# A decoder layer with 32 experts: the second product of each run worked among the pieces of the next run's first product, and pairs of experts on whole float32 weights

## The chip, the cores and the metric

The kernel runs on one NeuronCore of a Trainium2 chip. The metric is the device time of one execution in microseconds (us). Before the change it is 1546.03 us, the median of three runs (1543.41 to 1550.98). The engines are TensorE (PE; its weight loads are a row of their own, PEld), VectorE (DVE), ScalarE (ACT), GpSimd (POOL) and SyncE (SP), which issues the loads.

## The reference

One decoder layer on 512 tokens of width 1024: a mixer with two head groups, then a mixture of experts, then a per-layer embedding and a norm. The change concerns the experts alone. Every token goes to 4 of 32 experts; an expert takes the rows given to it through two products with a clamped, gated activation between them, and the results are summed per token by their gates.

```python
hh = jnp.dot(xs, w_gu[e]) + b_gu[e]              # (rows, 1024) x (1024, 2048)
glu, lin = jnp.split(hh, 2, axis=-1)
glu = jnp.minimum(glu, SWIGLU_LIMIT)
lin = jnp.clip(lin, -SWIGLU_LIMIT, SWIGLU_LIMIT)
act = glu * jax.nn.sigmoid(SWIGLU_ALPHA * glu) * (lin + 1.0)
return jnp.dot(act, w_dn[e]) + b_dn[e]           # (rows, 1024) x (1024, 1024)
```

All weights are float32. An expert's weights are 12 MB, those of all 32 are 384 MB, and each is read once.

## The kernel before

**Tiling.** The experts are sorted by the number of their tokens, the fullest first, and each rank has a fixed number of slots (CAPS): 128 for ranks 0 to 4, then 112, 96, 80 and 72, and 64 for the last twelve. Ranks 0 to 19 are worked alone (a single), ranks 20 to 31 two at a time (a pair; the two experts lie in the two 64-column halves of the PE array). RUNS is the order: run 0 is rank 0, runs 1 and 2 are pairs, 3 to 5 singles, 6 a pair, 7 to 10 singles, 11 a pair, 12 to 17 singles, 18 a pair, 19 to 24 singles, and 25 (LAST) a pair.

**Pieces.** An expert's weights are cut into 12 pieces of 1 MB (128 partitions x 2 x 1024 float32). Pieces 0 to 7 are the first product's (w_gu: 0 to 3 the gate half, 4 to 7 the linear half), 8 to 11 the second's (w_dn). The list jobs holds all pieces in the order of their use. SyncE loads them in this order into RAW, a ring of eight slots (issue, raw_slot, L770). A slot comes free again when its piece has been split or, for a piece used as it is, when PE has used it (done).

**Split and native pieces.** A split writes a piece as two float16 parts into HL, a ring of six slots: ScalarE writes the high part (L212, `hl<-raw`), VectorE the low part (L213). PE then takes three float16 products for one (mm3, L218 to L220). NATIVE says how many of an expert's last pieces are not split but multiplied in float32 straight from the raw slot: 4 for a rank with 64 slots (its second product), 0 for the others. advance runs the splits AHEAD = 4 places of the list ahead of the piece that PE takes.

**A run.** prep builds the one-hot matrix of the run's tokens and gather collects their columns on PE into xT (L1242, copied by ScalarE in L1244). up is the first product: for each half a bias product (L1276), then the pieces, then the activation (L1295 to L1300: glu, ln). In a pair, up runs once for each expert, each with 64 token columns. After up, prep of the next run; then down_t (or down for 128 slots, down2 for a pair: L1361) is the second product, into the PSUM tiles yT or y. y_out scales y by the gates into yh and yl (L1371, L1372). After every third run a combine adds three runs' results to the tokens (L1383, and acc in L1385); it is a generator that up works off a step at a time.

So in program order all of a run's first product comes first, then all of its second, and the next run starts behind it. A scheduler moves single instructions a little; the order that each engine really has is shown in the section on the change.

## Time and profile before

| what | value |
|---|---|
| median of three runs | 1546.03 us |
| the profiled execution | 1546.58 us |
| its span in the trace | 1544.8 us |
| PE busy | 1349.7 us, 87% |
| VectorE busy | 1216.5 us, 79% |
| ScalarE busy | 1012.2 us, 66% |
| bytes moved | 433.27 MB, 280 GB/s over the span |

The busy times are those of the profiled execution. The ends of products on PE are modelled by the profiler, so a PE that is shown busy need not be working at its full pace; the distance between the starts of products tells more. The page cuts the span into 40 slices of 38.6 us; the expert part begins in the ninth and ends in the thirty-ninth. The granted clock is a share of TensorE's 2.4 GHz.

### The profile page before, as it was taken

What the parts mean: (1) busy time and instruction counts of PE and PEld (TensorE: products, weight loads), DVE (VectorE), ACT (ScalarE), POOL (GpSimd) and SP (SyncE); (2) the same over time, 40 slices, a digit from 0 to 9 for tenths busy, and PEclk for the clock granted to TensorE, in tenths of its full rate; (3) what the DMA queues carried; (4) which work ended last, traced back from release to release, by engine and by line L of the source; (5) the groups of instructions that cost most, each with busy time, mean ns of one, the idle gap of its engine ahead of it and who ended that gap; (6) DMA issues with size and microseconds to landing.
All of it is one profiled execution on the core that took longest, in us unless ns stands there. A gap on an engine that the chain in (4) does not pass through costs nothing. (4 is left out here: it accounts for less than half of the span.)

```text
span 1544.8 us, 48662 instructions
## 1 busy us (share of the span) xinstructions
PE 1349.7 (87%) x21678; PEld 1060.3 (69%) x21678; DVE 1216.5 (79%) x1356; ACT 1012.2 (66%) x1156; POOL 49.2 (3%) x114
## 2 busy tenths in 40 slices
PE   7999899878889999899998899988887788798687
PEld 4766656466665787777797578878765777667447
DVE  7447876688595998769999299999975899988834
ACT  6458765557373777558688177777844767867634
POOL 2001000210000000000000000000000000000002
PEclk9999999879999999999999999999999999999799
DMA  7122130358999999889989789999997999998911
GB/s 244 51 86 83 56 110 29 110 188 276 340 379 364 410 408 336 312 321 408 391 308 380 269 325 408 395 340 374 352 328 278 408 381 343 311 350 289 359 66 56
DMA packets 124264, 433.27 MB, mean 280 GB/s; under 512 B 7977, under 2 KB 18770, under 8 KB 123986
## 3 DMA queue, kind: packets, MB, share of 16 engines
q1 hardware_dynamic: 123858, 429.85, 75.5%
q8 instruction: 171, 2.80, 0.7%
q14 instruction: 43, 0.35, 0.1%
q10 hardware_dynamic: 192, 0.26, 0.1%
HBM read 427.99 MB, written 2.10 MB: 278 GB/s over the span
## 5 line engine op out<-in xcount | busy, mean ns | idle before, releaser
L213 DVE SCALAR_TENSOR_TENSOR hl<-raw,hl 128x2048 f16<-128x2048 f32 x337 | 762.9, 2287 | 77.5 <-ACT hl L212 76.2
L212 ACT ACTIVATE hl<-raw 128x2048 f16<-128x2048 f32 x337 | 630.0, 1903 | 129.4 <-DMA raw<-in_w_gu_dram 57.8
L220 PE MATMUL hps<-xT,hl 128*128 128x64 f16 (+5 forms) x4096 | 493.4, 204 | 49.6 <-DVE hl L213 40.3
L218 PE MATMUL hps<-xT,hl 128*128 128x64 f16 (+5 forms) x4096 | 497.4, 204 | 12.5 <-issue 7.2
L219 PE MATMUL hps<-xT,hl 128*128 128x64 f16 (+5 forms) x4096 | 496.9, 204 | 8.6 <-issue 8.6
L220 PEld LDWEIGHTS <-hl 128*128 128x128 f16 (+1 forms) x4208 | 400.4, 100 | 76.0 <-DVE hl L213 53.6
L218 PEld LDWEIGHTS <-hl 128*128 128x128 f16 (+1 forms) x4208 | 403.0, 100 | 37.6 <-issue 10.8
L219 PEld LDWEIGHTS <-hl 128*128 128x128 f16 (+1 forms) x4208 | 403.1, 100 | 28.1 <-issue 12.0
L1342 PE MATMUL yT<-acts,hl 128*128 128x80 f16 (+3 forms) x960 | 120.7, 210 | 7.8 <-DVE acts L213 7.8
L1341 PE MATMUL yT<-acts,hl 128*128 128x80 f16 (+3 forms) x960 | 121.9, 209 | 1.7 <-ACT acts L212 1.6
L1343 PE MATMUL yT<-acts,hl 128*128 128x80 f16 (+3 forms) x960 | 120.6, 210 | 0.8 <-DVE hl L213 0.7
L1361 PE MATMUL y<-raw,ln 128*64 128x512 f32 x384 | 101.3, 611 | 11.4 <-DMA raw<-in_w_dn_dram 9.1
L1343 PEld LDWEIGHTS <-hl 128*128 128x128 f16 x960 | 98.2, 103 | 10.1 <-issue 8.9
L1341 PEld LDWEIGHTS <-hl 128*128 128x128 f16 x960 | 98.1, 103 | 3.2 <-issue 2.2
L1342 PEld LDWEIGHTS <-hl 128*128 128x128 f16 x960 | 98.4, 103 | 0.5 <-issue 0.3
L1372 DVE SCALAR_TENSOR_TENSOR yl<-y,gcl,yh 128x512 f16<-128x512 f32 (+4 forms) x52 | 37.7, 744 | 68.1 <-ACT yh L1371 67.5
L1383 PE MATMUL pg<-yh,ohT 128*128 128x512 f16 (+4 forms) x208 | 80.5, 389 | 10.5 <-issue 5.0
L1371 ACT ACTIVATE yh<-y,gcl 128x512 f16<-128x512 f32 (+4 forms) x52 | 35.0, 682 | 82.8 <-PE y L1361 71.0
L1244 ACT ACTIVATE xT<-pg 128x512 f16<-128x512 f32 (+4 forms) x104 | 51.7, 513 | 50.0 <-PE pg L1242 42.3
L1383 PE MATMUL pg<-yl,ohT 128*128 128x512 f16 (+4 forms) x208 | 80.7, 389 | 1.8 <-DVE yl L1372 1.7
L1361 PEld LDWEIGHTS y<-raw,ln 128*64 128x64 f32 x384 | 31.9, 139 | 67.5 <-issue 59.3
L1383 PEld LDWEIGHTS <-ohT 128*128 128x128 f16 (+4 forms) x416 | 38.5, 99 | 51.5 <-issue 23.4
(369 smaller groups left out, 2251.6 us busy)
## 6 DMA issues: line engine op xcount, KB each, us to landing
raw<-in_w_gu_dram SPq DMA_DIRECT2D x256, 1024.0 KB, 9.6
raw<-in_w_dn_dram SPq DMA_DIRECT2D x128, 1024.0 KB, 8.1
raw<-in_w_in_dram SPq DMA_DIRECT2D x2, 2048.0 KB
raw<-in_w_o_dram SPq DMA_DIRECT2D x2, 2048.0 KB
raw<-in_w_ple_gate_dram SPq DMA_DIRECT2D x4, 1024.0 KB
acc<-in_x_dram SPq DMA_DIRECT2D x4, 512.0 KB, 3.5
raw<-in_w_in_dram SPq DMA_DIRECT2D x4, 512.0 KB, 7.2
out_dram<-acc SPq DMA_DIRECT2D x8, 256.0 KB, 2.0
```

The source lines that it names most:

```text
L212: later["hl"] = (A.activation(hi, src, AF.Copy, scale=scale), V.scalar_tensor_tensor(lo, src, scale, hi, op0=OP.mult, op1=OP.subtract))
L213: V.scalar_tensor_tensor(lo, src, scale, hi, op0=OP.mult, op1=OP.subtract))
L218: PE.matmul(ps, ah, bh, start=first, stop=False, skip_group_check=True)
L219: PE.matmul(ps, ah, bl, start=False, stop=False, skip_group_check=True)
L220: PE.matmul(ps, al, bh, start=False, stop=last, skip_group_check=True)
L1244: A.activation((xT[:, h] if parts else xT)[:, q * 4:(q + 1) * 4, :c], ps[:, :4 * c].rearrange("p (k c) -> p k c", k=4), AF.Copy, scale=1.0 ...
L1341: PE.matmul(o[f], w[0][:, m, r], ah, start=first and f % 4 == 0, stop=False, skip_group_check=True)
L1342: PE.matmul(o[f], w[0][:, m, r], al, start=False, stop=False, skip_group_check=True)
L1343: PE.matmul(o[f], w[1][:, m, r], ah, start=False, stop=last, skip_group_check=True)
L1361: PE.matmul(y[n][e * 64:(e + 1) * 64], acts[e][:, 2 * q + m], ws[e][:, m, n * 512:(n + 1) * 512], start=q + m == 0, stop=q + m == 4, skip_ ...
L1372: V.scalar_tensor_tensor(yl[:c, s_], y[n][:c], gcl[:c], yh[:c, s_], op0=OP.mult, op1=OP.subtract)
L1383: PE.matmul(ps, ohT[:c, i * P:(i + 1) * P], y_[:c, n * 512:(n + 1) * 512], start=e == 0 and q == 0, stop=e == last and q == 1)
```

## The change

Four things change together.

1. The order. phase gives the order of the pieces in stretch r: run r's eight first-product pieces (u) with the four second-product pieces of run r - 1 (d) among them: u0 u1 d0 u2 d1 u3 u4 d2 u5 d3 u6 u7. The list of loads has the same order; in a pair each place stands for two pieces. up, down, down_t and down2 become generators that are stepped in this order. The next run's prep comes after u5.
2. Pairs take all 12 pieces in float32 (NATIVE 12 instead of 4), so none of a pair's pieces is split.
3. A pair's first product is turned round: up2 holds the tokens (xTf, 64 columns for each expert) in the array and streams 512 columns of weights, as the second product does. Its activations then come out with tokens on partitions, so turn2 transposes them (8 transposes on PE, two copies on ScalarE into actT) before the second product. The gather of a pair writes one float32 tile instead of two float16 ones.
4. A single's activations are split in one go (act_parts) at the end of its stretch, and y_out of run r comes in stretch r + 1, after d3 or, for ranks with fewer than 128 slots, after u6.

```diff
-NATIVE = {c: 0 if c == 128 else 4 if c <= 64 else 0 for c in CAPS}
+NATIVE = {c: 0 if c == 128 else 12 if c <= 64 else 0 for c in CAPS}
...
+def phase(r):
+
+    u = [("u", _q) for _q in range(8)] if r <= LAST else []
+    d = [("d", _q) for _q in range(4)] if r else []
+    return [u[0], u[1], d[0], u[2], d[1], u[3], u[4], d[2], u[5], d[3], u[6], u[7]] if u and d else u + d
...
-        jobs += [(s_, q) for s_ in us for q in range(8)]
-        if n_ == LAST:
+        if n_ > LAST:
             jobs += [("t", q) for q in range(4)]
-        jobs += [(s_, q) for q in range(8, 12) for s_ in us]
+        jobs += [(s_, q if u_ == "u" else 8 + q) for u_, q in phase(n_) for s_ in RUNS[n_ if u_ == "u" else n_ - 1]]
...
+    def pair_mm(ps, xT, k0, q, get, put, opened):
+
+        ws = [get(e, q) for e in range(2)]
+        whole = ws[0][0] is None
+        for m in range(2):
+            k = k0 + m
+            for n in range(2):
+                c = slice(n * 512, (n + 1) * 512)
+                for a, b in ((0, 0),) if whole else ((0, 0), (0, 1), (1, 0)):
+                    for e in range(2):
+                        PE.matmul(ps[n][E2[e]], xT[:, k, E2[e]] if whole else xT[:, a, k, E2[e]],
+                                  (ws[e][1] if whole else ws[e][1][b])[:, m, c], start=not opened and k == 0,
+                                  stop=k == KD - 1 and (whole or a == 1), skip_group_check=True)
+        for e in range(2):
+            put(e, q)
...
+            for q in range(4):
+                pair_mm(ps, xT, 2 * q, 4 * a + q, get, put, True)
+                step(2)
+                if q == 3:
+                    if a:
+                        acts[:] = [act_of(h, 512, g) for h, g in zip(ps, acts)]
+                    else:
+                        acts.extend(glu_of(h, 512) for h in ps)
+                yield
...
+    def turn2(acts):
+
+        t = mp.tile([P, KD, P], F32, name="actT", tag="acts", bufs=1)
+        for n in range(2):
+            ps = pg()
+            for f in range(4):
+                PE.transpose(ps[:, f * P:(f + 1) * P], acts[n][:, f * P:(f + 1) * P], identf)
+            A.activation(t[:, 4 * n:4 * n + 4].rearrange("p f t -> p (f t)"), ps, AF.Copy)
+        return t
...
+        for u_, q in phase(ns_):
+            if u_ == "u":
+                next(g_up)
+                if q == 0 and turned_:
+                    prev[2] = turn2(prev[2])
...
+                if q == 6 and g_down is not None:
+                    next(g_down)
+                    ended()
+                    g_down = None
+                if q == 5:
+                    at(ns_, 2)
+                    if ns_ < LAST:
+                        step(99)
+                        nxt = prep(RUNS[ns_ + 1])
+                continue
...
+            next(g_down)
+            if q == 3 and prev[5]:
+                ended()
+                g_down = None
```

The first place is ScalarE in run 11, the pair of ranks 24 and 25. Before, from the last yh of the single ahead of it (96x512) to the pair's own yh (128x512):

```order
L1371 ACTIVATE yh<-y,gcl 96x512
L212 ACTIVATE hl<-raw 128x2048 x4
L1300 ACTIVATE glu<-glu 128x512
L212 ACTIVATE hl<-raw 128x2048 x4
L1300 ACTIVATE glu<-glu 128x512
L212 ACTIVATE hl<-raw 128x2048
L1244 ACTIVATE xT<-pg 128x4x96 x4
L1262 ACTIVATE ohT<-ohT_ps 96x512
L1371 ACTIVATE yh<-y,gcl 128x512 x2
L212 ACTIVATE hl<-raw 128x2048 x7
```

In the change, from the yh of the single two runs ahead (112x512) to the yh of the single just ahead (96x512). The four hl rows are the splits of d0 to d3 of the single ahead, acts are that single's activations, and xT is the gather for the next run:

```order
L1432 ACTIVATE yh<-y,gcl 112x512 x2
L219 ACTIVATE hl<-raw 128x2048
L219 ACTIVATE acts<-ln 128x4x96 x2
L219 ACTIVATE hl<-raw 128x2048
L1274 ACTIVATE glu<-glu 128x512 x2
L219 ACTIVATE hl<-raw 128x2048
L1250 ACTIVATE xT<-pg 128x4x96 x3
L219 ACTIVATE hl<-raw 128x2048
L1250 ACTIVATE xT<-pg 128x4x96
L1268 ACTIVATE ohT<-ohT_ps 96x512
L1364 ACTIVATE yt<-yT 128x384 x2
L1432 ACTIVATE yh<-y,gcl 96x512 x2
```

The pair's own splits are gone, and the splits of the next run no longer stand behind a yh that needs all of the pair's second product.

The second place is VectorE one run later. Before, the pair's yl (128x512) is followed at once by the combine's additions (acc), and then by the glu of run 12 (96 slots: 128x384):

```order
L1372 SCALAR_TENSOR_TENSOR yl<-y,gcl,yh 128x512 x2
L1385 SCALAR_TENSOR_TENSOR acc<-pg,acc 128x512 x2
L213 SCALAR_TENSOR_TENSOR hl<-raw,hl 128x2048
L1385 SCALAR_TENSOR_TENSOR acc<-pg,acc 128x512 x2
L213 SCALAR_TENSOR_TENSOR hl<-raw,hl 128x2048 x2
L1385 SCALAR_TENSOR_TENSOR acc<-pg,acc 128x512
```

In the change run 12's glu comes first, then the pair's yl, and the additions go on past run 12's ln into the next run:

```order
L1273 TENSOR_SCALAR glu<-hps 128x384 x2
L220 SCALAR_TENSOR_TENSOR hl<-raw,hl 128x2048
L1433 SCALAR_TENSOR_TENSOR yl<-y,gcl,yh 128x512 x2
L1446 SCALAR_TENSOR_TENSOR acc<-pg,acc 128x512 x2
L220 SCALAR_TENSOR_TENSOR hl<-raw,hl 128x2048
L1446 SCALAR_TENSOR_TENSOR acc<-pg,acc 128x512
L220 SCALAR_TENSOR_TENSOR hl<-raw,hl 128x2048
L1446 SCALAR_TENSOR_TENSOR acc<-pg,acc 128x512
L220 SCALAR_TENSOR_TENSOR hl<-raw,hl 128x2048
L1280 TENSOR_SCALAR ln<-hps 128x384 x2
```

The combine of runs 9 to 11 has moved from the run behind the pair to the end of it and the run after.

## Rows read from the trace of the kernel before

**Rows 1.** The page: span, and VectorE's tenths and GB/s in 40 slices

```profile
span 1544.8 us, 48662 instructions
...
DVE  7447876688595998769999299999975899988834
...
GB/s 244 51 86 83 56 110 29 110 188 276 340 379 364 410 408 336 312 321 408 391 308 380 269 325 408 395 340 374 352 328 278 408 381 343 311 350 289 359 66 56
```

**Rows 2.** Stretches: length, busy PE PEld DVE ACT POOL, clock, DMA share, GB/s

```profile
373.00:537.00 164.00, 146.27 (x2468) 106.26 (x2466) 127.29 (x101) 97.93 (x74) 0.00 (x0) 0.98 0.97 366
537.00:611.00 74.00, 72.73 (x1033) 60.76 (x1031) 67.93 (x53) 57.62 (x47) 0.00 (x0) 1.00 0.97 375
611.00:711.00 100.00, 91.79 (x1504) 68.36 (x1503) 77.15 (x60) 59.64 (x47) 0.00 (x0) 1.00 0.91 334
711.00:829.00 118.00, 112.02 (x2113) 103.27 (x2111) 109.01 (x88) 91.38 (x79) 0.00 (x0) 1.00 0.96 365
829.00:933.00 104.00, 90.23 (x1619) 69.82 (x1620) 74.42 (x59) 56.98 (x48) 0.00 (x0) 0.95 0.85 321
933.00:1106.00 173.00, 155.35 (x3448) 143.59 (x3446) 162.69 (x134) 137.02 (x125) 0.00 (x0) 0.98 1.00 375
1106.00:1217.00 111.00, 89.48 (x1699) 68.90 (x1698) 79.23 (x62) 62.86 (x54) 0.00 (x0) 0.94 0.89 327
1217.00:1411.00 194.00, 163.55 (x3492) 139.62 (x3490) 174.34 (x145) 148.35 (x136) 0.00 (x0) 0.97 0.94 341
1411.00:1478.00 67.00, 48.34 (x798) 32.09 (x793) 49.99 (x61) 36.06 (x48) 0.00 (x0) 0.85 0.91 328
1478.00:1545.00 67.00, 52.68 (x466) 42.85 (x464) 33.31 (x56) 29.37 (x58) 11.10 (x21) 0.91 0.11 40
```

**Rows 3.** Groups by line and shape: busy us, mean ns, idle before

```profile
L213 DVE SCALAR_TENSOR_TENSOR hl<-raw,hl 128x2048 f16<-128x2048 f32 x337 | 762.9, 2287 | 77.5 <-ACT hl L212 76.2
L212 ACT ACTIVATE hl<-raw 128x2048 f16<-128x2048 f32 x337 | 630.0, 1903 | 129.4 <-DMA raw<-in_w_gu_dram 57.8 <-PE hps L219 23.5 <-PE hps L220 15.9
```

**Rows 4.** Shorter stretches, columns as in the second group

```profile
424.00:486.00 62.00, 53.53 (x981) 36.28 (x979) 45.71 (x38) 32.88 (x24) 0.00 (x0) 1.00 1.01 390
...
865.00:871.00 6.00, 4.46 (x34) 2.00 (x32) 1.18 (x4) 1.36 (x3) 0.00 (x0) 1.00 0.07 23
871.00:877.00 6.00, 6.00 (x31) 2.04 (x28) 0.00 (x0) 0.00 (x0) 0.00 (x0) 1.00 0.69 169
...
1451.00:1463.00 12.00, 5.56 (x10) 1.44 (x12) 9.99 (x24) 6.12 (x16) 0.00 (x0) 0.50 1.03 406
```

**Rows 5.** Timeline of SyncE's issues in run 11 (start, length, instruction)

```profile
839.87 19.67 SPq L770 DMA_DIRECT2D raw<-in_w_dn_dram  x8
871.45 25.99 SPq L770 DMA_DIRECT2D raw<-in_w_gu_dram  x8
```

**Rows 6.** Timeline of PE: first and last products of four streams

```profile
306.07 0.38 PE L218 MATMUL mm<-hl,mT 128*128 128x512 f16 x1
...
307.80 0.38 PE L220 MATMUL mm<-hl,mT 128*128 128x512 f16 x1
...
332.03 0.22 PE L219 MATMUL hps<-xT,hl 128*128 128x128 f16 x1
...
340.07 0.22 PE L219 MATMUL hps<-xT,hl 128*128 128x128 f16 x1
...
469.98 0.20 PE L220 MATMUL hps<-xT,hl 128*128 128x64 f16 x1
...
471.30 0.19 PE L220 MATMUL hps<-xT,hl 128*128 128x64 f16 x1
...
655.90 13.95 PE L1361 MATMUL y<-raw,ln 128*64 128x512 f32 x62
```

**Rows 7.** Timeline of ScalarE at the end of run 11, idle time in brackets

```profile
886.67 0.69 ACT L1371 ACTIVATE yh<-y,gcl 128x512 f16<-128x512 f32 x1 [17.35 <-PE y L1361]
```

**Rows 8.** Waits: who for whom, us in total, times, longest

```profile
ACT yh L1371 <- PE y L1361: 71.0, 11, 20.5
```

More of the change, by code (lines that the diff above doesn't have):

```diff
@@ L1277, in up @@
                           skip_group_check=True)
-            for k in range(KD):
-                q = 4 * a + k // 2
-                if k % 2 == 0:
-                    slot, w = get(q)
-                for f in range(KD):
-                    t, end = slice(f * P, (f + 1) * P), k == KD - 1
-                    if slot is None:
-                        PE.matmul(o[f], w[:, k % 2, t], xT[:, k, :c], start=False, stop=end, skip_group_check=True)
-                    else:
-                        xh, xl = (xT[:, b, k, x0:x0 + c] for b in range(2))
-                        mm3(o[f], w[0][:, k % 2, t], w[1][:, k % 2, t], xh, xl, False, end)
-                if k % 2:
-                    put(q)
-                step()
@@ L1308, in down, with act_parts, ybanks @@
+    def act_parts(acts, c):
+        t = mp.tile([P, 2, 2, 4, P], F16, name="acts", tag="acts", bufs=1)
+        r = [[t[:, j, b, :, :c] for b in range(2)] for j in range(2)]
+        for j in range(2):
+            hl(*r[j], acts[j], SX / S)
+        return r
+    def ybanks(name="y"):
+        return [py_.tile([P, 512], F32, name=name, tag="py") for _ in range(2)]
+    def down(get, put, acts, c, y):
+        y.extend(ybanks())
         for q in range(4):
@@ L1310, in down @@
             j = q // 2
-            if slot is not None and j not in split_acts:
-                split_acts[j] = [t[:, j, b, :, :c] for b in range(2)]
-                hl(*split_acts[j], acts[j], SX / S)
             for m in range(q % 2 * 2, q % 2 * 2 + 2):
@@ new lines, in down_t @@
+        yield
+    E2 = [slice(e * 64, (e + 1) * 64) for e in range(2)]
+    def pair_mm(ps, xT, k0, q, get, put, opened):
+        ws = [get(e, q) for e in range(2)]
+        whole = ws[0][0] is None
+        for m in range(2):
+            k = k0 + m
[8 more added lines that the diff above has]
+            put(e, q)
@@ new lines, in up2 @@
+    def up2(get, put, xT, brows, acts):
+        for a in range(2):
+            ps = [ph_.tile([P, 512], F32, name="hps2", tag="ph") for _ in range(2)]
+            for n in range(2):
+                for e in range(2):
+                    PE.matmul(ps[n][E2[e]], brows[e].to_broadcast([P, 64]),
+                              btab[:, a * D + n * 512:a * D + (n + 1) * 512], start=True, stop=False,
+                              skip_group_check=True)
+            for q in range(4):
+                pair_mm(ps, xT, 2 * q, 4 * a + q, get, put, True)
+                step(2)
+                if q == 3:
+                    if a:
+                        acts[:] = [act_of(h, 512, g) for h, g in zip(ps, acts)]
+                    else:
+                        acts.extend(glu_of(h, 512) for h in ps)
+                yield
@@ new lines, in turn2, with down2 @@
+    def turn2(acts):
+        t = mp.tile([P, KD, P], F32, name="actT", tag="acts", bufs=1)
+        for n in range(2):
+            ps = pg()
+            for f in range(4):
+                PE.transpose(ps[:, f * P:(f + 1) * P], acts[n][:, f * P:(f + 1) * P], identf)
+            A.activation(t[:, 4 * n:4 * n + 4].rearrange("p f t -> p (f t)"), ps, AF.Copy)
+        return t
+    def down2(get, put, actT, y):
+        y.extend(ybanks())
+        for q in range(4):
+            pair_mm(y, actT, 2 * q, 8 + q, get, put, False)
+            yield
@@ L1424, in put @@
                 pass
-            acts = up(get, put, xT, 0, br, P)
-            y = [py_.tile([P, 512], F32, name="y", tag="py") for _ in range(2)]
-            down(y, get, put, acts, P)
+            acts, y = [], []
+            list(up(get, put, xT, br, P, acts))
+            list(down(get, put, acts, P, y))
             list(combine([y_out(y, gcl, P) + (ohT, P)]))
```

154 lines of the change are left out of this document (77 added, 77 removed).

## The prediction

> **What bounds the kernel now.** I read the page's slices first. The expert part runs from the tenth slice to the third from last, and no engine is full there: VectorE's digits fall to 2, and the loads stand at 408 to 410 GB/s in five slices but at 269 to 340 in thirteen [rows 1]. A load of one piece (1 MB, 1.0486e6 bytes) takes 1.0486e6 / 408e9 = 2.57 us when nothing holds it up; mostly something does.
>
> Next, the table by stretches says where [rows 2]. I cut the part where a run's yh is written (run 0's at 373, run 25's at 1478) into nine stages, A to I, in the order of the rows; the tenth row is what follows. In the stages of single runs behind single runs (B, D, F, H: 74 + 118 + 173 + 194 = 559 us) VectorE is busy 514 of 559 us, and PE fills B (72.7 of 74). They go at the pace of the splits, which take 2.29 us each on VectorE and 1.90 on ScalarE, 337 of them [rows 3]. The stages with pairs (A, C, E, G) have VectorE busy only 358 of 479 us, and yet their loads run at 321 to 366 GB/s.
>
> The fine table shows the hole in E [rows 4]: between 865 and 871 us loads stand at 23 GB/s, and until 877 ScalarE and VectorE do next to nothing while PE works. The timelines give the cause. SyncE issues the pair's eight second-product loads from 839.9 on, the last by 859.5, and then nothing until 871.5 [rows 5]: all eight raw slots hold float32 pieces, which PE cannot use before the pair's activations exist, and when they do, PE needs some 14 us (13.95 for 62 of the 64 recorded products of the pair at 656) [rows 6]. ScalarE stands at yh for 17.35 us, with the next run's splits queued behind it [rows 7]; the waits view counts 71 us of this [rows 8].
>
> **The change, part by part.**
> *Splits.* Each of the 12 pair experts loses its 8 splits: 96 x 2.29 = 220 us off VectorE, 96 x 1.90 = 182 us off ScalarE [rows 3]. Per pair two ScalarE copies of the gather go and two actT copies come. This is only worth what lay on the path: VectorE bounds B, D, F and H, where no pair's split stood.
>
> *The pair's first product on PE.* A piece took 48 narrow products at a spacing of 1.32 us over 45 steps, 0.0293 us [rows 6], so two pieces cost 96 x 0.0293 = 2.8 us. Now two pieces have the shape and number of the second product's: 16 recorded products at 13.95 / 62 = 0.225 us, 3.6 us [rows 6]. A pair's PE work grows by 8 x 0.8 = 6.4 us, 38 us over six pairs: a loss, and PE is close to full.
>
> *The interleaving.* The holes close because the pair's second-product pieces now come two at a time between the next run's pieces, after their activations. The order above shows it: ScalarE has four splits in the pair's run, one by one between other work. Each stage must then be bounded anew by the largest of loads (pieces x 2.57, less what was loaded ahead, at most eight slots), VectorE and PE.
>
> PE's work I count from spacings [rows 6]: 8.04 us over 144 rows, 0.0558 us, at 128 columns; 0.0293 at 64; linear between them (an estimate); 1.73 us over 8, 0.216, at 512. A piece of a single's first product is 48 x 0.0558 = 2.68 us at 128 slots, 2.04 at 96, 1.72 at 80; the second product costs the same (2.6 at 128 slots); a gather 64 spacings and half a us; a combine 48 x 0.216 = 10.4; a run's bias, or a pair's transposes, about 1.
> - A (60 pieces): loads 154, less 13 for five slots filled ahead (none to eight is possible), 141. PE 44 (a pair's first product 28.8, run 0's second 10.4, gather, bias) + 53 (28.8, a second 14.4, bias, gather, and 3.5 for the output bias) + 42 (21.4, 14.4 and small ones) + half a combine, 144. So 144; it was 164.
> - B: PE 74, and the other half of that combine, which used to end in A: 79; it was 74. Loads get 17 ahead.
> - C (36 pieces): loads 92.5 - 17 = 75.5. PE 44.3 for the pair's run and 52.2 for the next with a combine: 96.5; it was 100.
> - D: VectorE's 109 at least, 118 before; 113. Loads get ahead by 18, all the slots hold.
> - E: loads 74.5. PE 42.2 + 35.6 = 78; it was 104. Its combine falls into F (the order's second place).
> - F: VectorE 163 and that combine's eight additions, 5; up to the old 173: 172.
> - G: loads 92.5 - 18 = 74.5. PE 40.5 + 43 = 83.5; it was 111.
> - H: between 174 and 194: 184.
> - I (the last pair's 16 and 8, run 24's 4, the gate's 4): 82 - 15 (two slots are kept for something else by then) = 67, as it was.
>
> Sum 144 + 79 + 96.5 + 113 + 78 + 172 + 83.5 + 184 + 67 = 1017 against 1105: -88 us. A, C, E and G (402 us) then go at PE's pace, and at the granted clock of such stages before, 0.95 and 0.94 in E and G [rows 2], they take 5.8% more, +23. Net -65. The profiled execution took 1546.6 (span 1544.8), half a us above the median of the three runs, 1546.0; so **1482 us**.
>
> What I cost at nothing: that SyncE's loads now wait on PE for native slots. Behind a waiting load stand only later loads; some four stay in flight, which is about what the eight slots give now. If fewer do, it goes the way of the second rival. The 67 us after yh stay [rows 2].
>
> **Bounds.** Below: D, F, H at VectorE's busy time (-4, -4, -10), no loss to the clock (-23): 1441. Above: D, F, H at their old times with F's combine (+5, +6, +10) and E and G winning half of what I book (+27): 1530.
>
> **The rivals.**
> 1. *PE falls to half clock, and the kernel gets slower.* Where PE has 3.6 us of work for each 5.14 us of loads, its granted clock may fall to 1.2 GHz. For it: from 1451 to 1463, with PE busy 5.6 of 12 us behind loads, the granted clock was 0.50 [rows 4]. Against it: A and C ran at 0.98 and 1.00, and PE's share will be higher. At half clock a step takes 7.2 us, longer than its loads, so PE itself sets the end. With a share s of the work of A, C, E and G done so, they take (1 + s) x 402; I booked s = 0.058; above s = 0.22 the 65 us are gone, and s = 0.5 gives 1482 + 0.44 x 402 = 1660 us. The Trainium skill, "TensorE: Matmul & The Clock Gate", Part 1, says that the throttled state is the default and that activity releases it; the trace agrees in the stretch just named. 12%.
> 2. *The loads don't hold 408 GB/s while all engines run.* A, B and F show 366 to 375 in the mean [rows 2]. At 373 a piece takes 2.81 us: A 155, E 89, G 98, I 79, the rest bound by PE and VectorE as above: +48, less 17 of the clock's loss where loads now cover it, 1513. Against it: 390 GB/s over 62 us of a pair's run [rows 4]. 8%. The Trainium skill has a rule that speaks harder against the change: "DMA: Bandwidth & Descriptors", Specifications, gives about 358 GB/s as the HBM limit of one core. By it the stages' 381 pieces would need 2.93 us each, 1117 us, more than the 1105 they take now, and nothing could be won; the slices at 410 GB/s disagree [rows 1].
> 3. *The wait moves into ScalarE's queue, and nothing changes.* In a pair's run each of four splits waits for its load with glu, xT or yh behind it. At up to one piece (2.57 us) each, 6 x 4 x 2.57 = 62 us come back: 1544. For it: ScalarE works strictly in its order and lost 71 us in this manner [rows 8]. Against it: loads arrive in the same order as the splits stand. 9%.
>
> **The numbers.** The forecast has 71%, and its own range is 1441 to 1530. About 8 us, half a per cent, is what a measurement of this kernel can tell from no change. Faster than 1538: the forecast and the second rival, 0.79. No change: the third, 0.09. Slower: the first, 0.12. The range that leaves out no more than 2 in 10 reaches from 1430 to 1548: it takes in the third rival, leaves out the first, and goes 11 us below the forecast's own, since PE's work in A and C is counted from an interpolated spacing.
>
> **What would show it.** 241 splits on VectorE. No stretch of 6 us below 100 GB/s in the pairs' runs of the middle, and ScalarE's wait for PE at yh under 15 us in all. E and G near 80 us, C nearly as long as before, PE's share of the span above 90%. I am wrong if the holes remain, if the granted clock in the pairs' stages falls under 0.8, or if B, D, F and H get longer because the moved pieces stand in their way.

## The result: 3% slower, and the profile after

| kernel | median | runs | ratio to before, 95% interval |
|---|---|---|---|
| before | 1547.33 us | 4 (1543.41 to 1550.98) | |
| after | 1595.88 us | 4 (1591.59 to 1599.95) | 1.0299 [1.0258, 1.0339] |

The forecast was 1482 us. The page of the changed kernel, against [rows 1] (the span is 1594.2 us); the last row is GB/s in 40 slices:

```profile
PE 1425.5 (89%) x17742; PEld 970.4 (61%) x17742; DVE 1010.4 (63%) x1260; ACT 837.4 (53%) x1060; POOL 49.5 (3%) x114
...
GB/s 254 32 83 81 74 86 80 1 245 298 383 355 360 364 390 273 311 350 407 398 262 336 359 361 406 369 353 304 249 334 293 407 404 325 318 276 235 292 97 54
```

PE has 76 us more to do than before (1349.7 us then), VectorE 206 us less. Loads reach 404 to 407 GB/s in four slices (before, 408 to 410 in five), and the mean over the span fell from 280 to 271 GB/s.

The stretches of the changed kernel, columns as in [rows 2]. A run's yh now comes in the next run's stretch, so I cut where the last activation of a run's first product ends (ln, L1281); stage I ends with the last yh of run 25. The nine rows are the stages A to I in their order.

```profile
362.00:534.00 172.00, 166.20 (x1206) 80.91 (x1202) 57.15 (x65) 44.30 (x45) 0.00 (x0) 1.00 0.94 351
534.00:610.00 76.00, 73.80 (x985) 59.19 (x984) 65.74 (x55) 50.38 (x42) 0.00 (x0) 1.00 0.93 358
610.00:716.00 106.00, 105.41 (x967) 59.58 (x964) 48.12 (x47) 40.06 (x40) 0.00 (x0) 1.00 0.91 327
716.00:827.00 111.00, 106.58 (x1800) 92.05 (x1798) 100.00 (x84) 79.90 (x68) 0.00 (x0) 1.00 0.97 369
827.00:933.00 106.00, 100.20 (x1053) 55.30 (x1050) 45.89 (x43) 38.42 (x39) 0.00 (x0) 1.00 0.91 327
933.00:1112.00 179.00, 158.39 (x3390) 141.97 (x3389) 164.16 (x138) 133.08 (x123) 0.00 (x0) 0.99 0.99 371
1112.00:1237.00 125.00, 111.29 (x1117) 58.46 (x1114) 48.80 (x48) 40.09 (x42) 0.00 (x0) 0.97 0.78 286
1237.00:1415.00 178.00, 148.99 (x3327) 129.13 (x3324) 162.05 (x135) 135.79 (x128) 0.00 (x0) 0.98 0.96 365
1415.00:1529.00 114.00, 86.88 (x461) 32.10 (x460) 38.90 (x64) 26.58 (x48) 0.00 (x0) 0.88 0.69 246
```

| stage | A | B | C | D | E | F | G | H | I |
|---|---|---|---|---|---|---|---|---|---|
| predicted, us | 144 | 79 | 96.5 | 113 | 78 | 172 | 83.5 | 184 | 67 |
| measured, us | 172 | 76 | 106 | 111 | 106 | 179 | 125 | 178 | 114 |

The rows sum to 1167 us, not 1017. Take off 11 us, because this cut begins at 362 and not at 373, and the 23 us booked for the clock: 116 us too long, and the forecast missed by 114. B, D, F and H, the single runs, are together 4 us shorter than predicted. All of the miss lies in the stages with pairs: A +28 (17 without the 11 us of the cut), C +9.5, E +28, G +41.5, I +47. The 23 us for the clock were not needed: the granted clock is 1.00 in A, C and E and 0.97 in G.

The groups by line, against [rows 3, 6] (columns as in the third group there):

```profile
L220 DVE SCALAR_TENSOR_TENSOR hl<-raw,hl 128x2048 f16<-128x2048 f32 x241 | 547.7, 2289 | 145.1 <-ACT hl L219 144.0
...
L1386 PE MATMUL hps<-raw,xTf 128*64 128x512 f32 x768 | 220.0, 615 | 14.2 <-DMA raw<-in_w_gu_dram 14.2
...
L1386 PE MATMUL y<-raw,actT 128*64 128x512 f32 x384 | 114.4, 611 | 3.1 <-DMA raw<-in_w_dn_dram 1.7 <-ACT actT L1418 1.4
```

The 241 splits are as predicted. But 48 steps of a pair's first product take 220.0 us of PE, 4.6 us each, and 24 of the second product 114.4 us, 4.8 each; I had counted 3.6.

Last, who waits for whom: SyncE's queue (SPq, the loads are L776), and ScalarE, against [rows 8].

```profile
SPq L776 <- DVE hl L220: 634.8, 197, 50.7
SPq L776 <- PE hps L1386: 80.3, 19, 17.4
SPq L776 <- DMA raw<-in_w_dn_dram: 59.2, 11, 12.2
SPq L776 <- DMA raw<-in_w_gu_dram: 58.8, 16, 8.4
```

```profile
ACT hl L219 <- DMA raw<-in_w_dn_dram: 78.1, 14, 16.8
...
ACT yh L1432 <- PE y L1386: 58.0, 11, 19.5
ACT hl L219 <- DMA raw<-in_w_gu_dram: 54.6, 18, 8.5
```

SyncE waits for splits most of the time, as it did before (690.5 us there), but it now also waits for splits whose own load has not landed (the two DMA rows, 118 us). ScalarE waits 132.7 us for loads, before 61.8. And it still stands at yh for 58.0 us in all: the wait that the order was to remove has shrunk from 71.0 us by 13.

### The profile page after: what moved, and what is told of

Read it like the earlier page. It is cut to its first block, busy times and chain, and to the rows that moved or that the text cites. A ratio compares the mean times of both kernels' runs of the same rounds, so it can differ in the third digit from the quotient of the medians.

```text
span 1594.2 us, 40340 instructions
## 1 busy us (share of the span) xinstructions
PE 1425.5 (89%) x17742; PEld 970.4 (61%) x17742; DVE 1010.4 (63%) x1260; ACT 837.4 (53%) x1060; POOL 49.5 (3%) x114
## 5 line engine op out<-in xcount | busy, mean ns | idle before, releaser
L220 DVE SCALAR_TENSOR_TENSOR hl<-raw,hl 128x2048 f16<-128x2048 f32 x241 | 547.7, 2289 | 145.1 <-ACT hl L219 144.0
L219 ACT ACTIVATE hl<-raw 128x2048 f16<-128x2048 f32 x241 | 451.0, 1903 | 145.6 <-DMA raw<-in_w_dn_dram 78.1
L227 PE MATMUL hps<-xT,hl 128*128 128x80 f16 (+4 forms) x2560 | 340.8, 209 | 30.8 <-DVE hl L220 26.7
L225 PE MATMUL hps<-xT,hl 128*128 128x80 f16 (+4 forms) x2560 | 353.4, 209 | 12.0 <-ACT hl L219 7.5
L226 PE MATMUL hps<-xT,hl 128*128 128x80 f16 (+4 forms) x2560 | 352.8, 208 | 1.4 <-issue 1.4
L227 PEld LDWEIGHTS <-hl 128*128 128x128 f16 (+1 forms) x2672 | 258.5, 99 | 63.2 <-DVE hl L220 46.0
L225 PEld LDWEIGHTS <-hl 128*128 128x128 f16 (+1 forms) x2672 | 262.7, 99 | 34.3 <-ACT hl L219 11.1
L226 PEld LDWEIGHTS <-hl 128*128 128x128 f16 (+1 forms) x2672 | 263.1, 99 | 18.2 <-issue 5.4
L1386 PE MATMUL hps<-raw,xTf 128*64 128x512 f32 x768 | 220.0, 615 | 14.2 <-DMA raw<-in_w_gu_dram 14.2
L1386 PEld LDWEIGHTS hps<-raw,xTf 128*64 128x64 f32 x768 | 64.1, 139 | 128.8 <-issue 106.3
L1386 PE MATMUL y<-raw,actT 128*64 128x512 f32 x384 | 114.4, 611 | 3.1 <-DMA raw<-in_w_dn_dram 1.7
L1359 PEld LDWEIGHTS <-hl 128*128 128x128 f16 x960 | 93.1, 100 | 25.5 <-DVE hl L220 17.8
L1357 PEld LDWEIGHTS <-hl 128*128 128x128 f16 x960 | 94.1, 100 | 15.4 <-issue 7.8
L1358 PEld LDWEIGHTS <-hl 128*128 128x128 f16 x960 | 94.6, 100 | 2.8 <-issue 2.0
L1274 ACT ACTIVATE glu<-glu 128x512 f32<-128x512 f32 (+4 forms) x52 | 27.6, 550 | 126.2 <-DVE glu L1273 126.2
L1250 ACT ACTIVATE xT<-pg 128x320 f16<-128x320 f32 (+4 forms) x80 | 38.1, 492 | 86.1 <-PE pg L1248 73.5
```

The source lines that it names most:

```text
L219: later["hl"] = (A.activation(hi, src, AF.Copy, scale=scale), V.scalar_tensor_tensor(lo, src, scale, hi, op0=OP.mult, op1=OP.subtract))
L220: V.scalar_tensor_tensor(lo, src, scale, hi, op0=OP.mult, op1=OP.subtract))
L225: PE.matmul(ps, ah, bh, start=first, stop=False, skip_group_check=True)
L226: PE.matmul(ps, ah, bl, start=False, stop=False, skip_group_check=True)
L227: PE.matmul(ps, al, bh, start=False, stop=last, skip_group_check=True)
L1250: A.activation((xT[:, h] if parts else xT)[:, q * 4:(q + 1) * 4, :c], ps[:, :4 * c].rearrange("p (k c) -> p k c", k=4), AF.Copy, scale=1.0 ...
```

## The experiments

Three theories stood at the start, as the first expectation names them; a fourth came with the second set of runs: that the split's place in ScalarE's queue, where it waits for its load with glu, xT and yh behind it, is the cause. All times are medians; the kernels marked "half" leave out products and so compute something else, and serve for their time alone. "Before" ran on the same chip as each kernel, and its medians there lay between 1548.7 and 1551.9 us.

| label | what it is | us | ratio to before, interval |
|---|---|---|---|
| e1_order_only | new order, pairs split | 1549.2 | 0.9995 [0.9972, 1.0018] |
| e2_whole_only | pairs whole, old order | 1563.3 | 1.0086 [1.0052, 1.0120] |
| e3_ahead8 | change, splits up to 8 ahead | 1716.6 | 1.1062 [1.1018, 1.1105] |
| e4_half_pair | change, half of the pairs' first product | 1583.1 | 1.0231 [1.0186, 1.0276] |
| e5_two_queues | change, whole pieces from GpSimd's queue | 1608.6 | 1.0382 [1.0355, 1.0409] |
| e6_ahead2 | change, splits up to 2 ahead | 1571.0 | 1.0130 [1.0094, 1.0165] |
| e6_swap2 | change, 10 load slots and 4 split slots | 1556.5 | 1.0046 [1.0027, 1.0064] |
| e7_singles_only | change, old order next to pairs | 1561.5 | 1.0066 [1.0045, 1.0087] |
| e8_late_slots | change, PE's slots asked for first | 1564.0 | 1.0089 [1.0066, 1.0112] |
| e8_late_swap2 | both of these | 1557.2 | 1.0046 [1.0024, 1.0069] |
| e9_before_swap2 | before, 10 and 4 slots | 1544.8 | 0.9968 [0.9947, 0.9988] |
| e9_order_swap2 | e1, 10 and 4 slots | 1549.3 | 0.9987 [0.9964, 1.0009] |
| e10_late_half | e8_late_slots, half of the first product | 1540.9 | 0.9926 [0.9901, 0.9951] |
| e10_whole_half | e2, half of the first product | 1541.6 | 0.9932 [0.9902, 0.9961] |
| e11_narrow | new order, the first product as before | 1544.8 | 0.9961 [0.9937, 0.9984] |
| e11_narrow_late | that, PE's slots asked for first | 1544.8 | 0.9958 [0.9933, 0.9983] |
| e11_narrow_swap2 | that, 10 and 4 slots | 1546.2 | 0.9957 [0.9932, 0.9982] |
| e12_all_split | new order, nothing whole | 1561.1 | 1.0051 [1.0027, 1.0076] |

### The two parts apart

**e1_order_only.**

```diff
-NATIVE = {c: 0 if c == 128 else 12 if c <= 64 else 0 for c in CAPS}
+NATIVE = {c: 0 if c == 128 else 4 if c <= 64 else 0 for c in CAPS}
-        return gather(..., parts=n == 1, mid=mid)
+        return gather(..., mid=mid)
```

> The order of the change is kept, and the pairs' first product takes split weights again (337 splits instead of 241, pair steps in half precision). Theory 1 (SyncE's one queue of loads is held up, because its next slot is freed by a split that stands behind other work on ScalarE and VectorE while PE has long freed later slots): the mixture of the two releasers is gone inside a pair's run and stays where second products are interleaved, so about half of the loss goes, 1570 us. Theory 2 (PE's float32 steps, 4.6 us each for 48 of them, set the pace): the steps become some 2.8 us, 48 x 1.8 = 86 us come back, 1510 us. Theory 3 (the interleaving costs by itself, whatever the weights): 1590 us or more.

**e2_whole_only.**

```diff
-    return [u[0], u[1], d[0], u[2], d[1], u[3], u[4], d[2], u[5], d[3], u[6], u[7]] if u and d else u + d
+    return d + u
...
```

This kernel also moves what hangs on the order: turn2 goes ahead of the second product, y_out to its end, and the next prep behind u7.

> The pairs take all weights whole in float32, and the order is undone: a run's second product comes ahead of the next run's first product, and its loads too. Theory 1: slots come free in the order in which SyncE asks for them again but for the seams between runs, so 1540 to 1560 us, the kernel before. Theory 2: the same float32 steps, so it stays near 1590 us. Theory 3: 1547 us or less, since 96 splits are gone.

Measured 1549.2 and 1563.3. Neither figure of theories 1 and 2 came: e1 is below the 1570 of the first and above the 1510 of the second, e2 is 3 us above the range of the first and far below the second. Theory 3 falls: the order alone costs nothing. It also wins nothing, and the whole weights alone lose 0.9%, though VectorE has 207 us less to do (1009.0 us busy in e2, 1216.5 before). Together they lose 3.0%, so 2.1 points (33 us) belong to neither part but to the two together. **e7_singles_only** puts the old order back next to pairs only:

```diff
+    if any(len(RUNS[n_]) > 1 for n_ in (r - 1, r) if 0 <= n_ <= LAST):
+        return d + u
...
```

> The change, but the interleaving only where both runs are single; a pair's run, and the run behind it, have the second product of the run before ahead of their first product, as in the kernel with the order undone (1563 us). Theory 1 and theory 4: nothing is mixed next to a pair, so the loss of the mixture, 1596 less 1563, goes: 1555 to 1570 us. If it is the interleaving of single runs that costs, 1590 us.

At 1561.5 us it is where the old order was (1563.3): interleaving singles is free, and the joint loss arises next to pairs. The stages of e8_late_slots, below, show next to which pairs.

### Is PE the bound, and where do the splits stand?

**e4_half_pair** leaves out the products of every other k in the pairs' first product.

```diff
             k = k0 + m
+            if opened and m == 0:
+                continue
```

> All of the change, but the pairs' first product leaves out every other 128 rows of the contraction (half of its products on PE); loads, splits and order as they are. Theory 2: 48 steps lose some 2.3 us each, 110 us, 1486 us. Theory 1: PE frees slots a little earlier, but the next load still waits for a split, so at most a quarter of that, 1570 to 1595 us.

1583.1 us: 13 us for a half (by the ratios 0.7 points, and the two intervals overlap), as theory 1 had it; PE's steps are not what costs the changed kernel most.

**e3_ahead8** and **e6_ahead2** change one number.

```diff
-AHEAD = 4
+AHEAD = 8
```

> All of the change, with each split put up to 8 pieces ahead of its use in the program (4 in the change), so that it stands earlier in the queues of ScalarE and VectorE and releases its slot earlier. Theory 1: a good part of SyncE's 635 us of waiting for VectorE's splits in the pairs' stretches moves away, 1550 to 1575 us. Theories 2 and 3: no change, 1590 to 1600 us.

> All of the change, with splits at most 2 pieces ahead of their use (4 in the change, 8 made it 1717 us). Theory 1: SyncE asks for PE's slots before those of the splits, 1550 to 1575 us. Theory 4: the splits stand later in ScalarE's queue and wait less, the same gain, 1550 to 1575 us; what tells them apart is whether SyncE's waits for VectorE (635 us) or ScalarE's for loads (133 us) shrink. If neither holds, the loss of lead costs the stretches of single runs and it is above 1596 us.

Eight made it 121 us slower, where I expected a gain; two made it 25 us faster. So theory 1 had its sign wrong. By the mark that e6_ahead2 was given beforehand, it spoke for theory 4: ScalarE's waits for loads shrank (132.7 to 45.6 us) and SyncE's for VectorE hardly (634.8 to 617.6). How theory 1 could still hold, with its sign turned, the program says: at u0 of a pair, advance already splits d0, four pieces on, and returns d0's slot to the free list; the slots of u0 and u1 return only behind their products. The next load in SyncE's queue then goes into d0's slot. It waits until d0 has landed and ScalarE and VectorE have split it, and every later load waits behind it, although PE has long given slots back. With 8 ahead ScalarE waits 229.7 us for loads.

The trace shows it best in run 25. SyncE's, ScalarE's, VectorE's and PE's timelines there:

```profile
1425.31 0.37 SPq L776 DMA_DIRECT2D raw<-in_w_dn_dram  x1
1425.93 16.47 SPq L776 DMA_DIRECT2D raw<-in_w_gu_dram  x4
1442.64 0.63 SPq L776 DMA_DIRECT2D raw<-in_w_dn_dram  x1
1443.51 17.39 SPq L776 DMA_DIRECT2D raw<-in_w_gu_dram  x2
1461.14 0.37 SPq L776 DMA_DIRECT2D raw<-in_w_dn_dram  x1
```

```profile
1433.67 1.91 ACT L219 ACTIVATE hl<-raw 128x2048 f16<-128x2048 f32 x1 [16.23 <-DMA raw<-in_w_dn_dram]
1453.77 0.63 ACT L1274 ACTIVATE glu<-glu 128x512 f32<-128x512 f32 x1 [18.18 <-DVE glu L1273]
...
1456.26 1.91 ACT L219 ACTIVATE hl<-raw 128x2048 f16<-128x2048 f32 x1 [1.01 <-DMA raw<-in_w_dn_dram]
```

```profile
1438.49 2.28 DVE L220 SCALAR_TENSOR_TENSOR hl<-raw,hl 128x2048 f16<-128x2048 f32 x1
1452.98 0.69 DVE L1273 TENSOR_SCALAR glu<-hps 128x512 f32<-128x512 f32 x1 [12.22 <-PE hps L1386]
...
1458.21 2.29 DVE L220 SCALAR_TENSOR_TENSOR hl<-raw,hl 128x2048 f16<-128x2048 f32 x1 [3.67 <-ACT hl L219]
```

```profile
1415.44 3.60 PE L1386 MATMUL hps<-raw,xTf 128*64 128x512 f32 x16
...
1438.56 1.93 PE L1386 MATMUL hps<-raw,xTf 128*64 128x512 f32 x4
...
1447.62 1.13 PE L1386 MATMUL hps<-raw,xTf 128*64 128x512 f32 x2 [5.19 <-DMA raw<-in_w_gu_dram]
```

ScalarE stands 16.23 us for a second-product piece that SyncE issued at 1425.31, and splits it at 1433.67; VectorE ends it at 1440.77. After the first of its four loads (1425.93) SyncE issues nothing until 1440.79; then the other three go out at once. PE, without weights, waits 5.19 us at 1447.62; glu waits for PE until 1452.98; and the next split, behind glu in ScalarE's queue, comes at 1456.26, and its slot with VectorE's end at 1460.50; SyncE, which has issued nothing since 1443.88, issues at 1460.53. One lap takes 20 us. Two short stretches, at the seam ahead of run 18 and in run 25, show what that does to the loads (last column, GB/s), with PE still busy on what had come before:

```profile
1113.00:1119.00 6.00, 5.75 (x59) 2.82 (x55) 0.31 (x2) 1.31 (x3) 0.00 (x0) 1.00 0.00 0
1436.00:1442.00 6.00, 5.67 (x57) 2.59 (x56) 3.58 (x3) 0.00 (x0) 0.00 (x0) 1.00 0.04 5
```

At the first of them SyncE issues nothing from 1108.9 to 1127.07. Its waits from 1100 to 1130, the longest 17.9 us, are for a split that ScalarE reaches at 1122.82, behind the gather's xT and ohT, which wait for PE.

### The order of the slots alone

**e8_late_slots** changes only which free slot a load gets: a split's slot goes to the free list once the whole pieces ahead of that split in the list of loads are done.

```diff
-                rawfree.append(f)
+                late.append((nsp, f))
+                freed()
...
+    late, undone = [], [n_ for n_, j in enumerate(jobs) if native(j)]
+
+    def freed():
+        while late and (not undone or late[0][0] < undone[0]):
+            rawfree.append(late.pop(0)[1])
...
             rawfree.append(raws.pop(j)[0])
+            undone.remove(jobs.index(j))
+            freed()
```

> All of the change with nothing moved on ScalarE, VectorE or PE; only the list of free slots differs: a split's slot is given to later loads once the program has passed the whole pieces that stand ahead of that split in the order of loads, so SyncE asks for PE's slots first. Theory 1 (the order in which SyncE asks for slots): 1550 to 1575 us, what shorter lead of the splits gave. Theory 4 (the splits' place in ScalarE's queue): no gain, 1590 us or more, since they stand where they stood.

1564.0 us, 2.1 points back, as much as the joint loss of the two parts, with the engines' work as it was (a scheduler moved a few neighbours, on ScalarE two splits by some rows and a few rows at the end). Theory 4, that the splits' place on ScalarE is the cause, falls: the splits stand where they stood, and ScalarE's wait for loads fell from 132.7 to 45.9 us by itself. SyncE's queue and ScalarE's waits in this kernel:

```profile
SPq L776 <- DVE hl L220: 480.8, 177, 51.0
SPq L776 <- PE hps L1395: 231.7, 62, 16.4
...
SPq L776 <- DMA raw<-in_w_dn_dram: 6.8, 1, 6.8
```

```profile
ACT hl L219 <- DMA raw<-in_w_dn_dram: 40.5, 10, 9.5
...
ACT hl L219 <- DMA raw<-in_w_gu_dram: 5.4, 3, 2.5
```

The waits have moved from VectorE and from the splits' own loads (118 us, now 7) to PE (the products of the pairs: 100 us in the change, now 346), which frees slots in the order in which they are asked for. SyncE in the same place of run 25:

```profile
1416.29 8.22 SPq L776 DMA_DIRECT2D raw<-in_w_gu_dram  x4
1424.76 0.37 SPq L776 DMA_DIRECT2D raw<-in_w_dn_dram  x1
1425.37 6.99 SPq L776 DMA_DIRECT2D raw<-in_w_gu_dram  x2
1432.60 0.57 SPq L776 DMA_DIRECT2D raw<-in_w_dn_dram  x1
1436.71 8.72 SPq L776 DMA_DIRECT2D raw<-in_w_gu_dram  x4
```

12 loads in 29 us, where the changed kernel issued 9 in 36. And the seam ahead of run 18, at nearly the same distance from the cut, has 302 GB/s instead of none. But the seams ahead of runs 6 and 11 are as empty as in the change, where they had 21 GB/s (602 to 608) and 8 (824 to 830); the first row is run 6's, and run 11's has 8 GB/s from 821 to 827:

```profile
599.00:605.00 6.00, 6.00 (x101) 5.62 (x101) 4.32 (x5) 3.06 (x3) 0.00 (x0) 1.00 0.01 5
...
1109.00:1115.00 6.00, 5.75 (x57) 2.95 (x56) 0.31 (x2) 1.31 (x3) 0.00 (x0) 1.00 0.94 302
```

Three of its stretches (E, G and I), with the same columns and the same cuts:

```profile
824.00:928.00 104.00, 99.89 (x1046) 55.03 (x1043) 45.77 (x42) 37.74 (x39) 0.00 (x0) 1.00 0.97 370
1107.00:1230.00 123.00, 112.48 (x1113) 59.78 (x1110) 48.84 (x47) 39.79 (x42) 0.00 (x0) 0.96 0.89 320
1406.00:1497.00 91.00, 74.94 (x460) 30.52 (x460) 37.89 (x62) 25.97 (x47) 0.00 (x0) 0.91 0.84 304
```

I went from 114 to 91 us, E and G by 2 each, A and H by some 3 and 2: 23 of 32 us are won in the last pair's stage, where two of the eight slots are kept for other data. In C, E and G together it is 4 us.

**e6_swap2** and **e8_late_swap2** turn two of the six split slots into load slots, without and with the late slots.

```diff
...
-    hlfree.extend(range(4))
+    hlfree.extend(range(2, 4))
+    rawfree.extend(range(8, 10))
```

> All of the change, with two of the six slots for split pieces turned into slots for loads (10 and 4 instead of 8 and 6). Theory 1: two more loads stand ahead of a held-up one, so a hole of some 10 us loses about 5 us in the pairs' stretches, 1560 to 1580 us, unless four slots are too few for the single runs. Theory 4: ScalarE's splits find their loads landed more often, 1570 us. If slots aren't what is short: 1596 us or more.

> The same with ten slots for loads and four for split pieces. Theory 1: the two gains overlap, since both close the same holes, 1540 to 1556 us. Theory 4: as with ten slots alone, 1556 us.

1556.5 and 1557.2: the first is below all that was expected, the second 1 us above theory 1's range and where theory 4 had it. With ten slots the order of the slots no longer matters. The holes that the two close are not all the same: at the seam ahead of run 18 e6_swap2 still has 0 GB/s (1101 to 1107). The last pair's stage is what both shorten, from 114 us to 91 (1398 to 1489 in e6_swap2), and 89 with both. The controls are **e9_before_swap2** and **e9_order_swap2**, the same edit on the kernel before and on e1:

> The kernel before with ten slots for loads and four for split pieces, as a control. If the shortage of slots is what the change made, 1540 to 1550 us, no change; if slots are short in the kernel before as well, the holes in its pairs' stretches shrink too, 1500 to 1530 us.

> The order of the change with the pairs' first product split (1549 us), with ten slots for loads and four for split pieces. All whole pieces are those of the pairs' second products here, so if slots are short wherever the two kinds are mixed, 1515 to 1540 us; if four split slots hold up the splits of the pairs' first product, 1550 us or more.

1544.8 and 1549.3: slots are not what the kernel before lacks, nor the order with split pairs. It is the whole first product, in the new order, that makes eight too few, and above all the six of the last pair.

**e5_two_queues** gives whole pieces a queue of their own.

```diff
-        SY.dma_start(v, ap)
+        (eng or SY).dma_start(v, ap)
...
+            nat = native((s_, q))
+            eng = G if nat else SY
...
-            f = rawfree.pop(0)
-            raws[s_, q] = f, raw_slot(f, views[s_][q])
+            f = next((f for f in rawfree if was.get(f, nat) == nat), rawfree[0])
+            rawfree.remove(f)
+            was[f] = nat
+            raws[s_, q] = f, raw_slot(f, views[v_][q], eng)
```

> All of the change, but the float32 pieces that PE takes whole are loaded by GpSimd's queue (idle in this part) instead of SyncE's, and a piece takes, if it can, a slot that a piece of its own kind used last. Theory 1, as the earlier runs leave it: the program frees a split's slot ahead of the slots that PE gives back, since the split is put up to 4 pieces before its use, so SyncE waits for the split while PE's slots lie free; with a queue of their own the whole pieces pass it, 1550 to 1570 us. Theory 4 (the split stands in ScalarE's queue, waits there for its load, and holds glu, xT and yh behind it): ScalarE's order is as it was, 1590 us or more.

1608.6 us, a miss for theory 1. It doesn't decide between the theories, since it changed more than I meant: SyncE's waits for PE's pair products rose from 100 to 290 us (pieces to be split got slots that PE held), and ScalarE waited 284.7 us for loads.

### What is left: PE's float32 steps

**e10_late_half** and **e10_whole_half** leave out the same half as e4, on e8_late_slots and on e2.

> The change with PE's slots asked for first (1564 us), and half of the products of the pairs' first product left out. If PE's float32 steps set the pace of the pairs' stretches once the order of slots is mended: 48 steps lose 1.8 to 2.3 us each where loads (5.1 us for a step) do not bound them first, so a good part of 86 to 110 us, 1490 to 1525 us. If loads or splits still set it, as in the change itself (13 us won): 1550 us or more.

> The order undone, the pairs whole (1563 us), and half of the products of the pairs' first product left out. If those float32 steps eat what the 96 splits gave: 1490 to 1530 us. If the eight slots do, since whole pieces no longer drain into the six slots for split ones: 1550 us or more.

1540.9 and 1541.6 us, 23 and 22 us less: between the two expectations each time. The groups of the pairs' first product in e8_late_slots and, below it, in e10_late_half:

```profile
L1395 PE MATMUL hps<-raw,xTf 128*64 128x512 f32 x768 | 210.7, 599 | 0.9 <-DMA raw<-in_w_gu_dram 0.9
```

```profile
L1397 PE MATMUL hps<-raw,xTf 128*64 128x512 f32 x384 | 144.4, 608 | 6.5 <-DMA raw<-in_w_gu_dram 6.5
```

66 us less of PE gave 23 us. PE's steps carry part of what was left, and not most of it. Stage E of e10_late_half, against 104 us in e8_late_slots:

```profile
821.00:920.00 99.00, 91.28 (x990) 52.82 (x987) 46.58 (x44) 38.45 (x39) 0.00 (x0) 0.98 0.99 381
```

**e11_narrow**, **e11_narrow_late** and **e11_narrow_swap2** keep the order and give the pairs' first product back its old form: split weights, 64 columns, up for one expert after the other within a step.

```diff
-NATIVE = {c: 0 if c == 128 else 12 if c <= 64 else 0 for c in CAPS}
+NATIVE = {c: 0 if c == 128 else 4 if c <= 64 else 0 for c in CAPS}
...
+        gens = [up(lambda q, e=e: get(e, q), lambda q, e=e: put(e, q), xT[:, :, :, E2[e]], brows[e], 64, parts_[e])
+                for e in range(2)]
+        for q in range(8):
+            for g_ in gens:
+                next(g_)
...
```

> The order of the change alone, with the pairs' first product in the kernel before's own form (split weights, 64 columns, one expert after the other within a step). Against the same order with wide split products (1549 us) PE has some 0.7 us less in each of 48 steps and no transposes of the pairs' activations. If PE bounds the pairs' stretches: 1510 to 1535 us, below the kernel before. If the mixture of slots or the splits do: 1545 us or more.

> The same with PE's slots asked for first. The only whole pieces are those of the pairs' second products, 48 instead of 144, so theory 1 gives a third of the 32 us that this won with the change: 5 to 12 us below the run without it. If that order matters only inside a pair's whole first product: no difference.

> The order of the change with the pairs' first product in the kernel before's form (1545 us), with ten slots for loads and four for split pieces. If slots that hold whole second-product pieces are what still limits its pairs' stretches (285 to 296 GB/s there), 1525 to 1540 us, the fastest of all; if PE or the splits are, 1545 us.

1544.8, 1544.8 and 1546.2: with 48 whole pieces instead of 144 neither the order of the slots nor more of them matters. The first is where its expectation had it for slots or splits, and not for PE; the second is the "no difference" of its expectation. These are the fastest kernels that compute the whole layer, by 0.4% over the kernel before, as is e9_before_swap2 by 0.3%. ScalarE still waits 60.0 us for PE at yh in e11_narrow, and its loads stand at 304 to 329 GB/s in C, E and G, cut as above (the 285 to 296 of the expectation are too low), so the order does not close the holes even with the cheap product.

**e12_all_split** goes the other way and splits the pairs' second product too. Against e11_narrow:

```diff
-NATIVE = {c: 0 if c == 128 else 4 if c <= 64 else 0 for c in CAPS}
+NATIVE = {c: 0 if c == 128 else 0 if c <= 64 else 0 for c in CAPS}
...
```

This kernel also splits the pair's activations in down2 and takes three float16 products for one there.

> The opposite of the change's second part: the order of the change, and the pairs take no weights whole at all, neither product. 48 more splits than in the kernel before on VectorE (2.29 us each, 110 us), no piece that waits for PE in a load slot, and some 1 us less of PE in each of 24 steps. If PE and the slots are what is scarce in the pairs' stretches: 1515 to 1540 us. If VectorE is: 24 splits and the rest of a pair then take as long as in a single run, some 2.8 us a piece, 1550 us or more.

1561.1 us, 0.9 points slower than e11_narrow: VectorE is then busy 1328 of 1559 us. So it came as expected for VectorE as the scarce engine, and not for PE and the slots.

## Why the prediction was wrong, step by step

**"That SyncE's loads now wait on PE for native slots", at nothing.** This step failed, and it is the largest loss that a single edit gives back: 32 of the 114 us, shown by e8_late_slots. The wait on PE itself was not what cost (it rose from 100 to 346 us there, and the kernel got faster). I wrote that behind a waiting load stand only later loads and that some four stay in flight. Behind it stood loads whose slots were free. What SyncE waits for is no longer one stream that frees slots in order: PE gives back whole pieces in its order, the splits theirs, and the program asks in a third order, that of the free list. I sent this to the second rival, loads slower by a tenth; it had a price of its own.

**Stage I, "67, as it was".** It took 114 us. I had bounded it by the loads and remembered the two kept slots only as loads ahead, not as slots missing. e8_late_slots gives back 23 of the 47, and ten slots the same; in the other stages with pairs the order of the slots is worth 3 us at most.

**PE's work in A, C, E and G, 402 us.** This step failed too: the work was mis-sized. It is 483 us busy (166.2 + 105.4 + 100.2 + 111.3 in the table of stretches); the stages last 509. So PE fills 95% of them, though a busy PE need not be at its pace. The PE groups of stage E show where:

```profile
L1386 PE MATMUL hps<-raw,xTf 128*64 128x512 f32 x122 | 32.5, 599 | 0.2 <-DMA raw<-in_w_gu_dram 0.2
L1386 PE MATMUL y<-raw,actT 128*64 128x512 f32 x64 | 20.6, 603 | 0.2 <-DMA raw<-in_w_dn_dram 0.2
...
L1444 PE MATMUL pg<-yh,ohT 112*128 112x512 f16 (+2 forms) x18 | 6.9, 381 | 0.2 <-DVE acc L1446 0.2
L1444 PE MATMUL pg<-yl,ohT 112*128 112x512 f16 (+2 forms) x18 | 6.8, 377 | 0.6 <-DVE yl L1433 0.6
```

The first product took 32.5 us, not 28.8; the second 20.6, not 14.4; and 36 rows of the combine, which I had put into F, lie in E, 7.8 us at the spacing of 0.216 in [rows 6]. That is 18 of the 22 us by which PE is busier than the 78 counted. The first two show in PE's rows of run 25 above: a whole step (16 recorded products) took 3.60 us, as I counted, but four products that stand between others took 1.93 us, where a quarter of a step is 0.9. The starts of the single records say why. In the step of 3.60 us the records start two at a time, a pair every 0.43 us; the four start one at a time (1438.56, 1439.04, 1439.47, 1439.90), so one record takes the place of two. In the whole changed kernel 168 of the 768 records of the first product and 104 of the 384 of the second start without a partner. The trace does not say which half of the array a record belongs to; that the partners are the two experts of a pair is a reading. The page of the kernel before had the price as well, 101.3 us for 24 steps, 4.2 each:

```profile
L1361 PE MATMUL y<-raw,ln 128*64 128x512 f32 x384 | 101.3, 611 | 11.4 <-DMA raw<-in_w_dn_dram 9.1
```

There 52 of the 384 records start alone, and [rows 6] shows a stretch in which nearly all go in pairs. That not all of this work sets the end is shown by the halves: 66 us of it gave 23.

**The loads ahead, 17 us in C and 18 in E and G.** GB/s times length, by 1.0486 MB for a piece, gives 33, 33 and 34 pieces loaded in C, E and G of the change, where 36 are used: the stages lived on a lead of 2 to 3 pieces, not 7. In E it is 37 in e8_late_slots and 36 in e10_late_half, so the stage used up no lead at all there; and 36 pieces at 408 GB/s are 92.5 us (an estimate). So with the order mended and half of the first product gone E still takes 99 us, at 381 GB/s: without a lead the loads alone put the 78 out of reach.

**The splits off VectorE.** 241, as predicted, and B, D, F and H came out at 544 us against 548. I said that the splits are only worth what lay on the path; e2 shows that what they were traded for cost 13 us more than they were worth, and no run takes the splits away without putting something in their place.

**The holes.** They moved: from the end of a pair's run [rows 4] to the seam ahead of it (0 GB/s from 1113 to 1119) and into the last pair (5 GB/s). That a hole costs its own length is not shown: e6_swap2 keeps the one ahead of run 18. ScalarE's wait at yh was 58.0 us, not under 15. The interleaving alone wins at most 0.4% (e11_narrow). E in e8_late_slots is still 104 us with loads at 370 GB/s and PE busy 99.9.

**The rivals.** The first, half clock, has the right sign and the wrong cause: the granted clock was 0.97 to 1.00 in A, C, E and G, and 0.88 in I. The second, loads below 408 GB/s while all engines run, is refuted as a cause: slices at 404 to 407 GB/s stand in the changed kernel too. The Trainium skill's figure of about 358 GB/s ("DMA: Bandwidth & Descriptors", Specifications) is passed there as it was before. The third, the wait moving into ScalarE's queue, is what the waits seem to show (132.7 us for loads), but e8_late_slots makes it a consequence: the loads came late, and ScalarE stood.

**What stays open.** With the order of the slots mended the change is at 1564 us, 82 above the forecast, and PE's halves account for 23 of these. E and G stay far above 78 and 83.5 us in every form of the pairs: E takes 106 us in the change, 101 in e1_order_only, 104 in e11_narrow, and took 104 before (cut at yh). The runs behind pairs stay long (run 19 takes 63 to 65 us from ln to ln in the change, e8_late_slots and e10_late_half, 60 in e2_whole_only, 52 in e1_order_only and 48 in e11_narrow). There ScalarE waits at xT for PE for 17.0 us in e8_late_slots, with splits behind; but at the same place of e1_order_only it waits 15.9 us, so this wait does not make the difference. What makes it stays open.

## What to carry to other kernels

A ring of load slots with one queue asks for slots in program order; when two engines give them back, compare the order of asking with the order of giving, and hand out first what comes free first. Look first where the ring is shortest: 23 of the 32 us of e8_late_slots came from the one stage where a pair has six slots, and with ten slots the order made no difference. A number that looks like a lead (AHEAD) sets the order too: 2, 4 and 8 gave 1571, 1596 and 1717 us. Before trading one engine's work for another's, sum the other engine's groups stage by stage, at the mean price of the whole kernel and not at that of its best stretch (4.2 and 3.6 us for a step here), and count loads ahead only where the trace shows them.

## What the runs showed that I had not expected

Float32 products for two experts in the two halves of the array keep 0.225 us per recorded product only where two records start together, every 0.43 us: 16 in 3.60 us, but 4 without partners in 1.93. Loads issued by GpSimd took 11.2 us from issue to landing (median of 96), those by SyncE in the same run 8.1 (160), with both queues in use.
